# The FFN down product of three layers by Strassen's seven block products, with the weight sums made on chip

## The chip, the cores and the metric

The kernel runs on all 8 cores of one Trainium2 chip. Each core computes half of one sequence of the batch (4 sequences of 8192 tokens). The metric is the device time in microseconds (us) of the slowest core. Most executions of one kernel agree within 0.3%. In some executions, whatever the kernel, one die (cores 0 to 3 or 4 to 7) or both are granted a lower TensorE clock and the time is several per cent longer. Those runs are called slow here, they are left out of every comparison, and where only one die was slow I also read the undisturbed die of the same run.

Names used below: PE is the matmul engine (TensorE), DVE is VectorE, ACT is ScalarE, POOL is GpSimd, SP is the engine that issues most plain DMAs. The "casting queue" is the DMA queue fed by GpSimd, which loads fp32 weights and writes them as bf16; the profile calls it q0 software_dynamic. The "hardware queue" is the one fed by SP, q1 hardware_dynamic; it copies without casting.

## The reference, cut to what matters

```python
def swiglu(h, w_gate, w_up, w_down):
    return (jax.nn.silu(h @ w_gate) * (h @ w_up)) @ w_down      # 1024 -> 2816 -> 1024

for i in range(4):                                   # DEPTH
    h = rmsnorm(x, mix_pre_g[i])
    m = mixer_a(h, ...) if i % 2 == 0 else mixer_b(h, ...)   # gMLP, pooling
    x = x + rmsnorm(m, mix_post_g[i])
    h = rmsnorm(x, ffn_pre_g[i])
    f = swiglu(h, ffn_w_gate[i], ffn_w_up[i], ffn_w_down[i])
    x = x + rmsnorm(f, ffn_post_g[i])
```

Input, output and weights are fp32. The kernel multiplies in bf16.

## The kernel before

A core goes through its tokens in 5 tiles of two halves (512, 400 or 384 tokens). Within a tile it runs the four layers, each a mixer and an FFN. While one half is in a vector phase (norms), the other half keeps PE busy. Programs for the engines are made by a list scheduler: each operation is a task with buffers that it reads and writes, and with a priority; each engine then executes its tasks strictly in the order that the scheduler chose.

All weights pass through one ring of six 1 MB slots. Cast weights come over the casting queue; one weight of mixer B (`w2_s`, folded on chip in tile 0 and stored as bf16) comes over the hardware queue.

```python
NSLOT = 6
class Piece:                       # one slot of the weight ring
    def __init__(self, src, cast=True, reads=(), k=None, parts=1):
        eng = "pool" if cast else "sp"
        ...
        t = t_dma(eng, (0, seq[0]), slot, src, list(reads), [var], ...)
        if last_load[0] is not None:
            t.preds[last_load[0]] = -1.0       # loads keep their order
...
BIG = [sb("BIG%d" % h, [128, 32 * HW[h]], BF16) for h in range(2)]
WSM = sb("WSM", [128, 1024], BF16)             # mixer A's constants: buffers of their own
BIAS = sb("BIAS", [128, 2048], F32)
w2_s = dram("w2_s", [2, 8, 128, 1024], BF16, "Internal")
...
def out_proj(s, v, loc, nk, rhs_fn, st, base, together=0, pr=None):
    for oc in range(KC):                       # 8 groups of 128 output channels
        b = bs[oc]                             # one PSUM bank each
        for i in range(0, nk, 8):
            mm_group(...)                      # nk matmuls of the half's width
        post_evac(st, v, s, oc, b)             # ACT: square for the norm, copy to MS
    st.rstd()                                  # statistics: squares summed on DVE,
                                               # one matmul with ONESM, Ln and Exp on ACT
...
# mixer B
pcs = [Piece(wb_in[j, q]) for q in range(2)]
tp = [Piece(w2_s[j].rearrange("k p n -> p k n")[:, :, q * 512:(q + 1) * 512], cast=False,
            reads=[("w2_s", j, kb) for kb in range(8)], k=8) for q in range(2)]
...
# mixer A
if t > 0:
    load_bias(j, s)                            # BIAS and WSM from DRAM, hardware queue
...
# FFN
pcs = [Piece(wf_gu[l, q]) for q in range(11)]
for pi in range(11):
    for h in hs:
        ffn_head(s, vout[h], pi, pcs[pi])      # gate, up, silu, product
tp = [Piece(wf_dn[l, q]) for q in range(6)]
for h in hs2:
    out_proj(s, v, by_block(tp, NJ), NJ, lambda k, v=v: bigfm(v, 0, k), st, 0)
    chain(v, s, st, gpost, nxt[h], ...)        # norm, residual, next norm -> H
```

## Time and profile before

| | before |
|---|---|
| time, median of 3 runs | 5720.78 us (5720.65 to 6790.34; the last is a slow run) |
| undisturbed die, by core | 5714.0 to 5718.3 us, granted clock 0.998 to 0.999 |
| PE busy on the profiled core | 5696.8 of 5754.8 us |
| PE idle between matmuls, median core | 20 us in tile 0, 16 in tiles 1 to 4 |
| time lost to half clock, median core | 9.5 us |

The last two rows are worked out from the trace: the idle time is the sum of all stretches between the first and the last matmul in which no matmul runs; the half-clock loss is half the time that the record of the granted clock shows at 0.5, whether PE had work in it or not. Tile 0 is taken to end at 1090 us.

The spans by core and their granted clock, before:

```profile
core 5: 5718.3 us, clock 0.998
...
die 0 (median of its cores): 5747.7 us, clock 0.992
die 1 (median of its cores): 5716.1 us, clock 0.999
```

Die 0 was slightly disturbed in this execution (stretches at 0.81), so the undisturbed die 1 is the yardstick: about 5716.

The groups of matmuls by shape on core 6, before. The number in front of the bar is the count; behind it come busy time, then the mean length of one (which overlaps its neighbours, so cost per matmul is busy time over count), then the idle time just before them:

```profile
L499 PE MATMUL ps<-BIG,WR 128*128 128x384 bf16 x7312 | 1208.4, 326 | 2.5 <-ACT SQ L480 0.8
```

That is 1208.4 / 7312 = 165 ns for a matmul of width 384, and hardly any waiting. What PE waited for on core 6, before (total us, times, longest):

```profile
PE ps L499 <- DVE SQF L601: 17.0, 7, 13.6
PE ps L499 <- DVE ACC L596: 7.4, 1, 7.4
PE ps L499 <- DVE H L641: 5.8, 5, 2.5
```

The longest of these are at the very start. Mixer weights and FFN weights don't appear in it (apart from 3.2 us for another mixer weight): in the kernel before, PE practically never waits for a DMA.

The timeline of PE and DVE-fed statistics at the hand-over from layer 2's FFN to layer 3's mixer B in tile 1, core 5 before (start, us, engine, line, operation, count, idle before):

```profile
2074.80 8.58 PE L499 MATMUL ps<-BIG,WR 128*128 128x512 bf16 x39
2083.22 2.97 PE L499 MATMUL ps<-WR,H 128*128 128x512 bf16 x13
2086.03 0.38 PE L499 MATMUL ps<-SQF,ONESM 128*128 128x512 bf16 x1
...
2095.75 8.44 PE L499 MATMUL ps<-BIG,WR 128*128 128x384 bf16 x48
...
2107.96 4.26 PE L499 MATMUL ps<-WR,H 128*128 128x512 bf16 x19 [0.82 <-DVE H L641]
```

The down product of the second half ends at 2083.3; its statistics matmul follows 2.7 us later; the mixer's output product, which uses `w2_s`, starts at 2095.75 without a wait; and the next half's input is ready 0.8 us late.

### The profile page before, as it was taken

Reading aid. Unit: us, or ns where it says so; the run is one execution under the profiler, and the core shown is the slowest. Engines: PE = TensorE matmul, PEld = TensorE weight load, DVE = VectorE, ACT = ScalarE, POOL = GpSimd, SP = SyncE. Lnnn points to the kernel's source line nnn. Section 1 sums busy time; section 2 is a strip of 40 time slices with the busy share of each in tenths; the row PEclk is TensorE's granted clock in tenths of the full one; section 3 lists DMA queues with packets and bytes.
Section 4 is the critical chain, followed back from the end, with each engine's and each line's share of the span. In section 5 each row is a group of like instructions: output and inputs, shape, how many; then the busy total and the mean of one; then the engine's idle time right before and its main releaser. Section 6 shows DMA issues by size and latency. Waiting matters only on the chain.

```text
span 5754.8 us, 92936 instructions; the slowest of 8 cores (5714.0 to 5754.8 us)
## 1 busy us (share of the span) xinstructions
PE 5696.8 (99%) x33311; PEld 3157.3 (55%) x33311; DVE 2630.8 (46%) x4841; ACT 2432.9 (42%) x5236; POOL 258.7 (4%) x492
## 2 busy tenths in 40 slices
PE   8999999999999999999999999999999999999999
PEld 4555555555555555555545555555565555555556
DVE  5453536352625454443436253524454444525352
ACT  5352635352525353533354253524534453525252
POOL 0000000000000000000000000000000000000000
PEclk9999999999999999999999999999999999999999
DMA  7856676664445545754544455655554676455544
GB/s 141 141 97 107 114 127 117 123 130 81 80 89 98 96 88 107 142 95 81 93 85 86 91 112 111 122 111 103 103 105 95 119 140 112 89 92 96 107 88 90
DMA packets 131409, 604.39 MB, mean 105 GB/s; under 512 B 12560, under 2 KB 55952, under 8 KB 67600
## 3 DMA queue, kind: packets, MB, share of 16 engines
q0 software_dynamic: 70272, 507.82, 51.1%
q1 hardware_dynamic: 60688, 90.63, 5.2%
q8 instruction: 276, 4.52, 0.3%
q14 instruction: 173, 1.42, 0.1%
HBM read 1082.53 MB, written 23.66 MB: 192 GB/s over the span
## 4 chain that ended last, share of the span: by engine, by line
PE 94%; DVE 2%; DMA 1%; ACT 1%; issue 1%; another core or an unknown queue 0%; DVEq 0%; SPq 0%; ACTq 0%; POOLq 0%
PE ps L499 94%; DMA MS<-xT 1%; DVE ACC L596 1%; DVE H L641 0%; DVE MS L688 0%; DMA WR<-wb_out 0%; ACT RS L622 0%; ACT BIG L480 0%; ACT RS L624 0%; DVE BIG L833 0%; DVE X L694 0%; ACT SQ L480 0%; DVE ACC L593 0%; ACT MS L480 0%; DMA X<-xT 0%
## 5 line engine op out<-in xcount | busy, mean ns | idle before, releaser
L499 PE MATMUL ps<-H,WR 128*128 128x384 bf16 (+2 forms) x16640 | 2967.7, 338 | 11.8 <-ACT SQ L480 4.3
L499 PEld LDWEIGHTS ps<-H,WR 128*128 128x128 bf16 x16640 | 1617.7, 98 | 1254.6 <-issue 24.7
L499 PE MATMUL ps<-BIG,WR 128*128 128x384 bf16 (+4 forms) x11056 | 1941.5, 337 | 2.1
L499 PEld LDWEIGHTS ps<-BIG,WR 128*128 128x128 bf16 x11056 | 1078.4, 98 | 832.8 <-issue 24.2
L750 DVE TENSOR_TENSOR BIG<-ps,SG 128x384 bf16<-128x384 f32 (+2 forms) x880 | 510.0, 585 | 1374.3 <-PE ps L499 1294.7
L480 ACT ACTIVATE SG<-ps 128x384 bf16<-128x384 f32 (+2 forms) x880 | 442.8, 513 | 1553.1 <-PE ps L499 1540.7
L596 DVE TENSOR_TENSOR ACC<-ACC,SQ 128x384 f32<-128x384 f32 (+2 forms) x730 | 428.7, 587 | 770.0 <-ACT SQ L480 706.7
L499 PE MATMUL ps<-WR,H 128*128 128x512 bf16 x3216 | 728.3, 386 | 12.8 <-DVE ACC L596 8.1
L480 ACT ACTIVATE MS<-ps 128x384 f32<-128x384 f32 (+3 forms) x648 | 324.5, 511 | 958.8 <-PE ps L499 947.6
L480 ACT ACTIVATE BIG<-ps 128x512 bf16<-128x512 f32 (+1 forms) x914 | 477.3, 561 | 338.2 <-PE ps L499 335.1
L499 PEld LDWEIGHTS ps<-WR,H 128*128 128x128 bf16 x3216 | 318.5, 99 | 402.7 <-issue 67.7
L688 DVE TENSOR_TENSOR MS<-MS,RS 128x384 f32<-128x384 f32 (+3 forms) x640 | 364.6, 580 | 200.0 <-ACT RS L624 199.9
L641 DVE SCALAR_TENSOR_TENSOR H<-X,GV,RS 128x384 bf16<-128x384 f32 (+2 forms) x576 | 330.0, 643 | 142.8 <-ACT RS L624 142.8
L480 ACT ACTIVATE SQ<-X 128x384 bf16<-128x384 f32 (+2 forms) x576 | 300.5, 549 | 200.9 <-DVE ACC L593 96.6
L694 DVE SCALAR_TENSOR_TENSOR X<-MS,GV,X 128x384 f32<-128x384 f32 (+2 forms) x560 | 354.6, 642 | 0.0
L480 ACT ACTIVATE SQ<-ps 128x384 bf16<-128x384 f32 (+3 forms) x648 | 321.9, 510 | 46.2 <-DVE ACC L596 29.2
L509 POOL DMA_DIRECT2D WR<-wf_gu x220 | 116.1, 528 | 2485.1 <-PE ps L499 2452.6
L593 DVE TENSOR_TENSOR ACC<-SQ 128x384 f32<-128x384 bf16 (+2 forms) x146 | 85.4, 585 | 189.4 <-ACT SQ L480 188.6
L480 ACT ACTIVATE SQ<-BIG 128x512 bf16<-128x512 bf16 x268 | 168.2, 638 | 7.1
L622 ACT ACTIVATE RS<-ps,EPSC 128x384 f32<-128x384 f32 (+2 forms) x152 | 92.6, 609 | 139.2 <-PE ps L499 139.1
L864 DVE SCALAR_TENSOR_TENSOR ACC<-ps,GV,BIAS 128x384 f32<-128x384 f32 (+2 forms) x184 | 107.5, 587 | 57.9 <-PE ps L499 54.8
L480 ACT ACT_TABLE_LOAD x94 | 120.6, 1283 | 19.7 <-PE ps L499 14.1
(63 smaller groups left out, 1555.9 us busy)
## 6 DMA issues: line engine op xcount, KB each, us to landing
WR<-wf_gu POOLq DMA_DIRECT2D x220, 1024.0 KB, 10.5
WR<-wf_dn POOLq DMA_DIRECT2D x120, 1024.0 KB, 9.0
WR<-wa_in POOLq DMA_DIRECT2D x79, 1024.0 KB, 14.3
WR<-wa_out POOLq DMA_DIRECT2D x40, 1024.0 KB, 10.0
WR<-wb_in POOLq DMA_DIRECT2D x20, 1024.0 KB, 10.1
WR<-w_s SPq DMA_DIRECT2D x20, 1024.0 KB, 10.2
yT<-MS SPq DMA_DIRECT2D x56, 192.0 KB, 16.6
X<-xT SPq DMA_DIRECT2D x48, 192.0 KB, 18.5
```

The costliest lines, as they stand in the source:

```text
L480: return e.activation(out=out() if callable(out) else out, in_=in_() if callable(in_) else in_, func=func, **kw)
L499: return e.matmul(out(), lhsT=lhsT() if callable(lhsT) else lhsT, rhs=rhs() if callable(rhs) else rhs, start=start, stop=stop)
L509: return e.dma_start(out=out() if callable(out) else out, in_=in_)
L593: t_dve(self.prio + (1,), lambda e: e.tensor_tensor(out=acc, in0=o0(), in1=o(), op=ALU.add), [k0, kq], ka, v.n)
L596: d = t_dve(self.prio + (1,), lambda e: e.tensor_tensor(out=acc, in0=acc, in1=o(), op=ALU.add), [kq] + ka, ka, v.n)
L622: t.insts.append((lambda e: e.activation(out=r, in_=bank(b, 0, v.n), func=AF.Ln, bias=EPSC[:]), [b, ("EPSC",)], kr, d_act(v.n)))
L641: t_dve(CH + (s, v.p, 1), lambda e, o=o, a=a, g=g, r=r: e.scalar_tensor_tensor(out=o, in0=a, scalar=g, in1=r, op0=ALU.mult, op1=ALU.mult), ...
L688: t_dve(CH + (s, v.p, 0), lambda e: e.tensor_tensor(out=m, in0=m, in1=r, op=ALU.mult), kf("MS", v, fc) + kr, kf("MS", v, fc), v.n)
L694: t_dve(CH + (s, v.p, 0), lambda e: e.scalar_tensor_tensor(out=o, in0=m, scalar=g, in1=x, op0=ALU.mult, op1=ALU.add), kf("MS", v, fc) + kf ...
L750: t_dve((0, s, v.p), lambda e, o=o, sg=sg, bu=bu: e.tensor_tensor(out=o, in0=bank(bu, 0, v.n), in1=sg(), op=ALU.mult), [bu, ksg], ko, v.n)
L864: t_dve((0, s, v.p, 0), lambda e, b=b, o3=o3, bb=bb, lg=lg, x0=x0, nl=nl, n=n: e.scalar_tensor_tensor(out=o3, in0=bank(b, x0 - v.c0, nl * ...
```

## The change

The intent: in layers 0 to 2 of tiles 1 to 4, do the down product [tokens x 2816] @ [2816 x 1024] as a 2x2x2 block product by Strassen's scheme, with seven half-size block products in place of eight. Each matmul then has half the width (192, 200 or 256 tokens), and there are 308 of them per half in place of 176. The seven combinations of weight blocks are made once, in tile 0, by DVE from the bf16 pieces that are in the ring anyway, and stored as bf16 in DRAM (`dn_s`); later tiles load them over the hardware queue. The token-side combinations are made by DVE after each gate/up piece. The last layer, and tile 0, keep the plain product (with its blocks in another order).

The diff, cut to its core:

```diff
+AB = (0, 22272)
+FB = (0, 19712)
+EXT = 16384
...
-    BIG = [sb("BIG%d" % h, [128, 32 * HW[h]], BF16) for h in range(2)]
+    BIGA = sb("BIG", [128, AB[1] + 32 * WB], BF16)         # one buffer for both halves
...
-    NSQ, NSG = 3, 3
+    NSQ, NSG, NT = 3, 4, 3
+    TB = [sb("TB%d" % i, [128, 512], F32) for i in range(NT)]
-    WSM = sb("WSM", [128, 1024], BF16)
-    BIAS = sb("BIAS", [128, 2048], F32)
+    BIAS = BIGA[:, EXT:EXT + 4096].bitcast(F32)            # now lies in the FFN's region
+    WSM = BIGA[:, EXT + 4096:EXT + 5120]
+    dn_s = dram("dn_s", [3, 2, 128, 154 * 128], BF16, "Internal")
...
+    def g_sums(s, v, kk):                                  # token-side sums, per gate/up piece
+        t_dve(pr, ... garr(v, 0, kk, 1) + garr(v, 4, kk, 1) ...)
+        t_dve(pr, ... garr(v, 4, kk, 1) - garr(v, 1, kk, -1) ...)
+        t_dve(pr, ... garr(v, 0, kk) + garr(v, 1, kk) ...)
...
+    def down7(s, v, gp, st7, st, rank, last):              # one group of outputs, one half
+        m4 = z.product(pr + (0, 0), z.q, m, unit(0, 0, 10), rg(5), True, alloc=z.pq)
+        z.product(pr + (0, 1), z.q, m, unit(0, 10), rg(5), False)
+        z.m4_taken((0, s, v.p, 0), m)                      # ACT copy PSUM -> TB
+        z.product(pr + (1,), z.p, m, unit(1), rg(4), True).preds.setdefault(m4, 0.0)
+        z.add_to_t((0, s, v.p, 0), z.p, m)                 # DVE: TB += PSUM
+        z.product(pr + (2,), z.r, m, unit(2), rg(6), True, alloc=z.r)
+        z.add_to_t((0, s, v.p, 0), z.r, m)
+        z.product(pr + (3,), z.q, m, unit(3), rg(0), False)   # then ACT copy to MS
+        z.product(pr + (4,), z.p, m, unit(4), rg(1), False)   # then ACT copy to MS
+        z.product(pr + (5,), z.q, m, unit(5), rg(2), False)   # then MS = TB - PSUM, two squares
+        z.product(pr + (6,), z.p, m, unit(6), rg(3), False)   # then MS = TB - PSUM, two squares
...
+    def stage(s, l, jobs, claimed):                        # tile 0: the weight sums
+        for fn, n, src, dsts in jobs:                      # 5 per piece of wf_dn
+            t = Task("dve", (1, s))
+            t.alloc = var                                  # one of five staging buffers in BIG
+            ...
+            for c0, nn, dst, key in dsts:
+                t_dma("sp", (0, s), dst, ...)              # store to dn_s
...
+            if keep:                                       # t > 0 and l < 3
+                dn7 = [Stream(dn_s[l, g], 154, ...) for g in (0, 1, 0)]
+                for rank, (i, g, last) in enumerate(((0, 0, False), (0, 1, True), (1, 1, False), (1, 0, True))):
+                    down7(s, vlast[h], g, dn7[(0, 1, 1, 2)[rank]], sts[h], rank, last)
+            else:
+                ...                                        # plain product, as before
+                if t == 0 and l < 3:
+                    for q in range(6):
+                        setup_dn(s, l, q, tp[q], claimed)
```

`BIAS` and `WSM` lose their own buffers, because the extra token-side arrays need the room. The cut also leaves out four further parts of the change: the scheduler's model of DMA time (one shared server for both queues in place of one for each), `dynamic_dma_scratch_size=8192` in the program's set-up, another order of blocks in the plain down product that is kept, and the loss of a separate buffer (`SQF`) for the last sum of the statistics.

## The prediction

> **What bounds the kernel now.** TensorE. The page shows PE busy 5697 of 5755 us (99%), the chain that ended last is 94% PE, the granted clock was 0.99 to 1.00 on all cores. PE waits total 58 us, some 25 at the start. Only PE work removed, or PE waits added, moves the time; DVE (46%), ACT (42%) and DMA have room.
>
> **Removed.** The FFN down product of tiles 1 to 4 in layers 0 to 2: 12 sub-layers of two halves, 176 matmuls per half. The groups by shape give PE time per matmul: 221 ns at width 512, 172 at 400, 167 at 384, 110.8 at 256, 64 at 144. Strassen does 308 matmuls per half at half the width. The narrow ones of the last sub-layer (256, 144) run almost in proportion, so I interpolate 84 ns at 192, 87 at 200. Per half: 512: 39.0 -> 34.1 us; 400: 30.3 -> 26.7; 384: 29.3 -> 25.9. Per layer: two halves of 512, one of 400, five of 384; in all 91 us, 1.6%. An ideal 7/8 would be 95; the rest is the fixed cost of 3168 more matmuls. The Trainium skill, "TensorE: Matmul & The Clock Gate", section "Wait — 56ns, not 53.3ns?", states about 2.5 ns each, an estimated 8 us; the trace roughly agrees (110.8 at 256, 106.7 of it streaming).
>
> **Added.** (a) DVE: three bf16 sums per gate/up piece and half, an estimated 0.7 to 1.3 us, under 12.4 us of PE work: off the path. (b) Evacuation: per output group two additions and two subtractions on DVE (0.55 to 0.69 us each), three copies on ACT (0.5 to 0.6). While the second half projects at 384, DVE has the first half's chain, 18.7 us, plus 9 for combining and statistics, against 25.9 us of PE; before it was 23 against 29. So that chain ends about when PE needs H, and the second half's starts behind: I expect 10 to 20 us of PE wait in all, most in tiles 3 and 4. (c) DMA: 15.1 MB of bf16 per down stage for 6.3 MB cast from fp32. 8 KB packets took 322 ns on the hardware queue (407 GB/s over 16 engines), 636 on the casting queue. A 1 MB piece needs an estimated 2.6 us, PE eats one in 2.7 to 3.5, six slots give about a quarter-stage of lead: no lasting stall. (d) Tile 0: 90 DVE sums (an estimated 0.6 us each) and 30 MB of stores; slots are held longer: 0 to 8 us.
>
> **Critical path.** 5721 - 91 + 15 (waits) + 4 (tile 0) = **5649 us**, range **5622 to 5690**. Chances: faster by over 2% (below 5606) 0.03, since even the ideal is 95 us; within 2% 0.94; slower 0.03.
>
> **What would show it.** Groups by shape: 7392 matmuls of width 192, 200, 256 at 84, 87, 111 ns, 4224 wide ones fewer; PE busy about 5606. Waits: PE for DVE H and for ACT or DVE evacuations up by 10 to 20 us, none large for DMA. Hardware queue about 300 MB, casting queue about 430. Granted clock unchanged.
>
> **What would make it wrong.** PE stalls at the products of 22 matmuls (1.8 us) because evacuations are late: 336 products, 0.2 us each would be 67 us. Weights arriving late, because one group's five pieces hold five of six slots for two quarters. Denser weight loads lowering the granted clock.

## More of the kernel before

`w2_s` is read with `[:, :, q*512:(q+1)*512]`, so each partition's 8 KB come as eight separate rows of 1 KB. And `BIAS` has a buffer of its own, so its load can be issued at almost any time.

The page of the profiled execution of the kernel before (its core 1), whole lines from the parts on engines, queues, the chain that ended last, and DMA issues (count, KB each, median us from issue to landing):

```profile
span 5754.8 us, 92936 instructions; the slowest of 8 cores (5714.0 to 5754.8 us)
...
PE 5696.8 (99%) x33311; PEld 3157.3 (55%) x33311; DVE 2630.8 (46%) x4841; ACT 2432.9 (42%) x5236; POOL 258.7 (4%) x492
...
q0 software_dynamic: 70272, 507.82, 51.1%
q1 hardware_dynamic: 60688, 90.63, 5.2%
...
PE 94%; DVE 2%; DMA 1%; ACT 1%; issue 1%; another core or an unknown queue 0%; DVEq 0%; SPq 0%; ACTq 0%; POOLq 0%
...
WR<-w_s SPq DMA_DIRECT2D x20, 1024.0 KB, 10.2
```

PE is busy 99% of the span, and the chain that ended last is PE for 94%. Nothing else is near its limit. The queue lines give packets, MB and the share of the 16 DMA engines' time.

## The result, and the profile after

| | before | after |
|---|---|---|
| median of the 5 runs | 5721.86 us (5720.65 to 6790.34) | 5809.21 us (5785.89 to 6701.45) |
| fast runs | 5720.65, 5720.78, 5721.86 | 5809.21, 5792.50, 5785.89 |
| after over before | | 1.0131, 95% interval 1.0105 to 1.0157 |

A ratio here and below is the mean time of one kernel's fast runs over the mean of the other's fast runs of the same rounds, so it isn't quite the ratio of the medians quoted. The change is correct, and it costs 1.3%: inside the 2% band, but outside the predicted range and on the other side.

The same lines of the page, after (its core 6, the slowest):

```profile
span 5807.7 us, 99963 instructions; the slowest of 8 cores (5745.1 to 5807.7 us)
...
PE 5599.6 (96%) x36271; PEld 3372.2 (58%) x36479; DVE 2999.6 (52%) x5915; ACT 2424.7 (42%) x5192; POOL 220.2 (4%) x420
...
q0 software_dynamic: 59904, 432.32, 43.5%
q1 hardware_dynamic: 107776, 302.60, 15.6%
...
PE 83%; DMA 8%; ACT 3%; DVE 3%; issue 2%; SPq 0%; another core or an unknown queue 0%; DVEq 0%; ACTq 0%; POOL 0%; POOLq 0%
...
WR<-w_s SPq DMA_DIRECT2D x20, 1024.0 KB, 27.6
```

The PE work did shrink, and the bytes moved as forecast. But the chain that ended last has lost 11 points of PE and gained 7 of DMA, and `w_s` (the same 20 loads of the same megabyte, by a line that the change does not touch) takes 27.6 us to land in place of 10.2.

The spans by core, after:

```profile
core 6: 5807.7 us, clock 0.990
...
die 0 (median of its cores): 5752.4 us, clock 0.994
die 1 (median of its cores): 5784.3 us, clock 0.991
```

The groups of matmuls by shape on core 6, after:

```profile
L540 PE MATMUL ps<-BIG,WR 128*128 128x384 bf16 x4672 | 788.1, 330 | 58.2 <-DMA WR<-w_s 42.0 <-DVE BIG L827 8.1 <-ACT SQ L521 5.7
...
L540 PE MATMUL ps<-BIG,WR 128*128 128x192 bf16 x4620 | 386.0, 246 | 0.8 <-DMA WR<-dn_s 0.5 <-ACT MS L521 0.4
...
L540 PE MATMUL ps<-BIG,WR 128*128 128x256 bf16 x2024 | 225.2, 273 | 0.0
```

A width of 192 costs 386.0 / 4620 = 83.5 ns, 256 costs 111.3 ns; with the 81.3 us of width 200, and without the 19.5 us of the 176 matmuls of width 256 that were there before, the new product costs 386.0 + 225.2 + 81.3 - 19.5 = 673 us. The forecast was 673. And these matmuls hardly wait. The 58.2 us are in front of a *different* product, the plain ones of width 384.

What PE waited for on core 6, after:

```profile
PE ps L540 <- DMA WR<-w_s: 42.0, 7, 7.3
PE ps L540 <- ACT SG L521: 26.1, 17, 12.4
PE ps L540 <- DVE H L688: 23.7, 13, 2.9
...
PE ps L540 <- DVE SQ L644: 17.8, 9, 13.4
PE ps L540 <- DVE BIG L827: 15.5, 6, 6.4
```

Three new waits: for `w_s`; for a silu result (`SG`) or the product of it (`BIG L827`), which is the gate/up stage; and for `H`, the next stage's input.

**The sum.** On the median core of each (of the undisturbed die, for before):

| us | before | after |
|---|---|---|
| PE busy (the rest) | 5655 | 5602 |
| PE idle between matmuls | 35 | 131 |
| before the first and after the last matmul | 26 | 27 |
| span | 5716 | 5760 |
| half-clock loss, as defined above | 9.5 | 35.5 |
| of it, while PE was busy | 3 | 21 |

Idle time rose by 96 us. Busy time should have fallen by 91 and fell by 53. Of these missing 38 us, 18 went to matmuls at half clock; the rest of the half-clock loss falls on stretches in which PE had nothing to do, where it costs nothing more. A matmul that stands alone after a gap shows its whole length of some 326 ns, not the 165 that it adds in a row, and the busy time lies in some 170 pieces after and some 80 before: an estimated 90 x 0.16 = 14 us. About 6 us are not traced. The cores also spread: core 6 has 181 us idle and a half-clock loss of 59.5 us (30 while PE was busy), and the slowest core is what is timed. About 12 of its 181 us are probably not real: on cores 0 and 6 some 200 matmul records are missing (the page counts 36271 matmuls and 36479 weight loads), and in the kernel before these two cores show 25 and 28 us in tiles 1 to 4 where the others show 12 to 16.

**Where the clock goes.** After a gap of some microseconds the granted clock is mostly 0.5 for 3.4 us or more. The windows on core 6 after, at the hand-over to layer 3's mixer B in tile 1 (window, length, then busy time and count of PE, PEld, DVE, ACT, POOL, then granted clock, DMA share, GB/s):

```profile
2120.00:2130.00 10.00, 9.78 (x82) 5.34 (x81) 7.32 (x12) 7.29 (x15) 0.00 (x0) 1.00 0.99 169
2130.00:2138.00 8.00, 0.90 (x11) 0.53 (x8) 7.14 (x12) 4.24 (x10) 0.00 (x0) 0.76 1.01 285
2138.00:2145.00 7.00, 7.00 (x36) 3.83 (x35) 0.32 (x1) 0.92 (x3) 0.00 (x0) 0.79 0.07 22
```

In the second window PE is idle for 7 us while all 16 DMA engines are busy; in the third PE runs 36 matmuls in 7.00 us, 194 ns each in place of 165, because the clock was granted at half speed for part of it. A 7 us gap costs 7 us, and then some more. The Trainium skill, "TensorE: Matmul & The Clock Gate", section "What's actually happening", says that an idle window of about 3.4 us takes the clock to half. The trace agrees on the unit: the 17 stretches on core 6 (118.9 us in all) last 3.41, 6.83 or 10.24 us, but for the one at the end. It does not agree that only gaps of that length count: on the eight cores, 58 of the 66 gaps over 3.4 us were followed by such a stretch, but so were 37 of the 104 gaps of 1.7 to 3.4 us, and 3 of the 154 of 0.8 to 1.7 us.

**Cause 1: a load in small packets, beside casts.** The chain on core 6 after, around the same place (start, us, what):

```profile
2107.58 29.67 DMA WR<-w_s
```

The load of `w_s` was issued at 2107.58 and took 29.67 us. PE had nothing to do from 2130.3 on and started when it landed:

```profile
2137.38 12.29 PE L540 MATMUL ps<-BIG,WR 128*128 128x384 bf16 x64 [7.10 <-DMA WR<-w_s]
2152.56 7.71 PE L540 MATMUL ps<-WR,H 128*128 128x512 bf16 x35 [2.88 <-DVE H L688]
```

(That is core 6's timeline of PE; the second line is a cause that comes further down.) Why 29.67 us? I counted the records of single DMA packets on core 6 in both traces, at this hand-over, where two loads of `w_s` make 2048 packets of 1 KB:

| core 6 | window, us | 1 KB packets, hardware queue | 8 KB packets, casting queue |
|---|---|---|---|
| before | 2063 to 2071 | 306 | 128 |
| before | 2071 to 2080 | 1742 | 0 |
| after | 2116 to 2132 | 357 | 299 |
| after | 2132 to 2138 | 1533 | 33 |

As long as casts are queued, the small packets go at about one for each cast packet, and hardly move; once the casts have run out, 1533 of them are through in 6 us. The Trainium skill, "DMA: Bandwidth & Descriptors", section "Queues, rings and completion order", says that each DMA engine takes turns between the queues that have work, packet by packet; the 357 to 299 agree, if each record of the trace is one such packet (the page's packet can hold several descriptors). A queue with 1 KB packets beside one with 8 KB packets then gets about an eighth of the bytes: here 357 KB of 2749. In the kernel before, this load was issued 30 us ahead of its use (2063.69 for 2093.24) with one cast beside it. After, it is issued 23 us ahead (2107.58 for 2130.3), and four casts and the load of `BIAS` (issued at 2105.17) are in flight with it. Why the issue comes later I did not test; the last load of `dn_s`, in front of it in the ring's order, is issued only at 2097.86.

**Cause 2: `BIAS` now loads at the hand-over.** Its memory lies in the FFN's region, so its load can't be issued before the last changed FFN of a tile is over. That is exactly where `w_s` is wanted, on the same queue, and `BIAS` goes first: from 2108 to 2116 us the hardware queue moved 125 packets of 8 KB and only 21 of 1 KB.

**Cause 3: the sums of tile 0 stop DVE.** DVE's timeline in tile 0 on core 6 after, and the PE line that follows from it:

```profile
282.30 0.57 DVE L827 TENSOR_TENSOR BIG<-ps,SG 128x400 bf16<-128x400 f32 x1 [2.15 <-PE ps L540]
299.38 0.69 DVE L978 TENSOR_TENSOR BIG<-WR 128x1024 bf16<-128x1024 bf16 x1 [16.51 <-DMA dn_s<-BIG]
...
301.84 0.57 DVE L827 TENSOR_TENSOR BIG<-ps,SG 128x400 bf16<-128x400 f32 x1
```

```profile
303.15 5.05 PE L540 MATMUL ps<-BIG,WR 128*128 128x400 bf16 x15 [7.64 <-ACT SG L521]
```

L978 is a weight sum. It waits 16.51 us for its staging buffer, whose store to `dn_s` (packets of 2 KB on the hardware queue, beside casts) hasn't landed. Behind it in DVE's order stands L827, the last product of the gate/up stage, which was ready all the time; PE waits for it. "DVE has room" (52% busy) is true and beside the point: an engine that runs in order stops at its first unready instruction. On core 6 the sums waited 66.5 us in all.

**Cause 4: a longer tail at the hand-over.** The groups end with a subtraction and two squares at once, where the plain product ended with one square. This is in the 23.7 us of waits for `H`; E1 below shows it undisturbed.

**Cause 5: the prefetch of the next tile's tokens** also comes in small packets (1.5 KB) on the hardware queue. After tile 0 the slowest of its loads took 34 to 47 us to land, by core, and some cores show a gap of PE there, of up to 12.4 us (at most 3.9 in one piece before). The landing itself isn't new: in the kernel before, the slowest took 42 to 52 us. What the change took away is the time that they had; why, I did not trace.

### The profile page after: what moved, and what is told of

Same layout as the page of the kernel before. It is cut to its first block, busy times and chain, and to the rows that moved or that the text cites. A ratio compares the mean times of both kernels' runs of the same rounds, so it can differ in the third digit from the quotient of the medians.

```text
span 5807.7 us, 99963 instructions; the slowest of 8 cores (5745.1 to 5807.7 us)
## 1 busy us (share of the span) xinstructions
PE 5599.6 (96%) x36271; PEld 3372.2 (58%) x36479; DVE 2999.6 (52%) x5915; ACT 2424.7 (42%) x5192; POOL 220.2 (4%) x420
## 3 DMA queue, kind: packets, MB, share of 16 engines
q0 software_dynamic: 59904, 432.32, 43.5%
q1 hardware_dynamic: 107776, 302.60, 15.6%
## 4 chain that ended last, share of the span: by engine, by line
PE 83%; DMA 8%; ACT 3%; DVE 3%; issue 2%; SPq 0%; another core or an unknown queue 0%; DVEq 0%; ACTq 0%; POOL 0%; POOLq 0%
PE ps L540 83%; DMA WR<-w_s 3%; DMA dn_s<-BIG 2%; DMA MS<-xT 1%; DVE H L688 1%; DMA WR<-wa_in 1%; ACT BIG L521 1%; ACT SQ L521 1%; ACT RS L666 1%; DMA WR<-wf_dn 1%; ACT L521 0%; DVE MS L736 0%; ACT RS L668 0%; DVE ACC L638 0%; ACT L651 0%
## 5 line engine op out<-in xcount | busy, mean ns | idle before, releaser
L540 PE MATMUL ps<-BIG,WR 128*128 128x384 bf16 (+5 forms) x14196 | 1850.5, 292 | 69.0 <-DMA WR<-w_s 42.0
L540 PEld LDWEIGHTS ps<-BIG,WR 128*128 128x128 bf16 x14224 | 1304.8, 98 | 590.6 <-issue 103.0
L540 PE MATMUL ps<-WR,H 128*128 128x512 bf16 x3142 | 711.6, 382 | 48.6 <-DVE H L688 20.4
L521 ACT ACTIVATE MS<-ps 128x384 f32<-128x384 f32 (+4 forms) x552 | 274.0, 509 | 766.2 <-PE ps L540 760.7
L736 DVE TENSOR_TENSOR MS<-MS,RS 128x384 f32<-128x384 f32 (+3 forms) x640 | 362.6, 577 | 174.9 <-ACT RS L668 174.7
L827 DVE TENSOR_TENSOR BIG<-ps,SG 128x384 bf16<-128x384 f32 (+2 forms) x352 | 199.3, 573 | 455.6 <-PE ps L540 402.2
L742 DVE SCALAR_TENSOR_TENSOR X<-MS,GV,X 128x384 f32<-128x384 f32 (+2 forms) x560 | 352.7, 637 | 0.0
L521 ACT ACTIVATE SQ<-ps 128x384 bf16<-128x384 f32 (+4 forms) x456 | 221.5, 505 | 52.0 <-DVE ACC L638 33.5
L521 ACT ACTIVATE SQ<-MS 128x384 bf16<-128x384 f32 (+2 forms) x256 | 130.7, 545 | 144.9 <-DVE MS L912 73.8
## 6 DMA issues: line engine op xcount, KB each, us to landing
WR<-w_s SPq DMA_DIRECT2D x20, 1024.0 KB, 27.6
```

What stands on the lines that cost most here:

```text
L521: return e.activation(out=out() if callable(out) else out, in_=in_() if callable(in_) else in_, func=func, **kw)
L540: return e.matmul(out(), lhsT=lhsT() if callable(lhsT) else lhsT, rhs=rhs() if callable(rhs) else rhs, start=start, stop=stop, skip_group_ ...
L736: t_dve(CH + (s, v.p, 0), lambda e: e.tensor_tensor(out=m, in0=m, in1=r, op=ALU.mult), kf("MS", v, fc) + kr, kf("MS", v, fc), v.n)
L742: t_dve(CH + (s, v.p, 0), lambda e: e.scalar_tensor_tensor(out=o, in0=m, scalar=g, in1=x, op0=ALU.mult, op1=ALU.add), kf("MS", v, fc) + kf ...
L827: t_dve((0, s, v.p), lambda e, o=o, sg=sg, bu=bu: e.tensor_tensor(out=o, in0=bank(bu, 0, v.n), in1=sg(), op=ALU.mult), [bu, ksg], ko, v.n)
```

## The experiments

My theory: the time went to waits that the change makes *outside* the new product (causes 1 to 5), multiplied by the clock. The rival, from the prediction: DVE has too much to do in the new product and falls behind. A second rival: the loads of `dn_s`, 3.3 times the traffic on the hardware queue, disturb everything else.

Eighteen runs in five groups; each group ran on one chip beside the kernel before. The kernel before measured 5718.97 to 5725.45 us in its fast runs, but for three that were mildly disturbed (5746 to 5778). Three edits recur, so I name them.

Edit R ("rows"): the layout of `w2_s`, so that a load has rows of 8 KB. Same bytes, same order of work.

```diff
-    w2_s = dram("w2_s", [2, 8, 128, 1024], BF16, "Internal")
+    w2_s = dram("w2_s", [2, 2, 128, 4096], BF16, "Internal")
-            const_dma(w2_s[j, kb], so, ...)
+            const_dma(w2_s[j].rearrange("q p (k n) -> p k q n", k=8)[:, kb], so.rearrange("p (q n) -> p q n", q=2), ...)
-            tp = [Piece(w2_s[j].rearrange("k p n -> p k n")[:, :, q * 512:(q + 1) * 512], cast=False, ..., k=8) ...]
+            tp = [Piece(w2_s[j, q], cast=False, reads=[...]) for q in range(2)]
```

Edit B ("bias later"): `load_bias` waits for a point inside the next stage, and so is issued behind `w_s`.

```diff
-    def load_bias(j, s):
-        t_dma("sp", (1, s), BIAS, bias_s[j], [("bias_s", j)], KBIAS, ...)
+    def load_bias(j, s, gate):
+        t_dma("sp", (1, s), BIAS, bias_s[j], [("bias_s", j)] + gate, KBIAS, ...)
-            if t > 0:
-                load_bias(j, s)
+            if t > 0 and l == 0:
+                load_bias(j, s, blocks(1, 5 * HW[1], 128))
+                ...                     # l > 0: after the second block of mixer A
```

Edit T ("short tail"): for the half whose statistics are on the path, the last two squares go straight to PE, which adds them up in PSUM, in place of two more additions on DVE.

```diff
+            if self.split and i >= KC - 3:
+                if i == KC - 3:
+                    d = t_dve(..., acc + square, ...)
+                    self.sum = Var("pss")
+                t_pe(..., [(bank(b), ONESM[:], o, i == KC - 3, last, ...)], ...)
+                return
+                        split=kind == 1 and t > 0 and l < 3 and v.p == 1)
```

### The change again, unedited (after_again)

> The changed kernel itself, unaltered, on the chip of this call, so that the edits beside it have a partner of the same rounds. Both theories: about 1.3% over before (5785 to 5810 us), TensorE idle 115 to 180 us per core, 24 to 48 us of it before the 384-wide matmuls on BIG and WR, half-clock time 65 to 120 us per core.

Measured: correct, 4 fast runs of 5789.95 to 5809.53 us, ratio 1.011 [1.0054, 1.0167]; `w_s` landed in 25.7 us; idle on the median core 37.5 us in tile 0 and 97.5 in tiles 1 to 4. The result holds on another chip.

### E1: edit R alone (e1_w2_rows)

> Only the layout of w2_s in DRAM: rows of 8 KB per partition in place of eight rows of 1 KB; the order of all instructions is the same. Theory (the small packets of the hardware queue take turns, one for one, with the 8 KB packets of the casting queue): landing of the w_s loads falls from 27.6 us (median) to about 12, the TensorE idle before the 384-wide matmuls on BIG and WR falls from 24-48 us per core to under 10, and with the half-clock stretches behind those gaps the time falls by 30 to 60 us against the changed kernel. Rival (the loads are issued too late because the slots come free late, or the bandwidth of the memory is used up): landing stays above 20 us and the time moves by less than 10 us.

Measured: correct, fast runs 5752.09, 5759.89 and 5765.55 us; ratio 1.0034 [0.9947, 1.0121]. The interval is wide because the kernel before had two mildly disturbed runs in this group; read against the undisturbed 5719 it is 0.6 to 0.8% longer. `w_s` in E1's DMA issues:

```profile
WR<-w_s SPq DMA_DIRECT2D x20, 1024.0 KB, 17.4
```

And the group of width 384 in E1, core 6, which had 58.2 us of idle time in front of it:

```profile
L540 PE MATMUL ps<-BIG,WR 128*128 128x384 bf16 x4672 | 774.6, 327 | 9.8 <-ACT SG L521 5.6 <-ACT BIG L521 3.7
```

The wait for `w_s` is gone from it altogether, with nothing changed but the layout of `w2_s` and with it the size of a packet (the traces of core 1 show every engine's instructions in the same order), and the time fell by some 40 us (mean of the fast runs 5800 to 5759). By core, the median landing was 23.3 to 27.8 us in the change and is 12.1 to 17.4 us here. That confirms cause 1. It also speaks against the second rival: the traffic of `dn_s` is all still there. `w_s` still takes longer than in the kernel before (7.9 to 10.2 us by core): `BIAS` is still in front of it.

E1 lets cause 4 be seen alone. PE, DVE and ACT at the same hand-over, E1, core 2:

```profile
2102.86 9.77 PE L540 MATMUL ps<-BIG,WR 128*128 128x256 bf16 x88
...
2112.73 0.69 DVE L918 TENSOR_TENSOR MS<-TB,ps 128x512 f32<-128x512 f32 x1
...
2113.52 1.15 ACT L521 ACTIVATE SQ<-MS 128x512 bf16<-128x512 f32 x2 [1.18 <-DVE MS L918]
...
2116.56 0.38 PE L540 MATMUL ps<-SQ,ONESM 128*128 128x512 bf16 x1
```

The last product ends at about 2112.5 (where the matmuls on `WR,H` begin), the statistics matmul comes at 2116.56: 4.1 us later, in place of 2.7. The subtraction (0.69), two squares (1.15) and the additions behind them stand in a row. PE's wait for `H` at this hand-over is 2.67 us here, 0.82 before.

### E2: hold the sums back until the gate/up stage is over (e2_stage_gate)

```diff
+                    gate = [k for h in hs for f in (NJ // 2 - 1, NJ - 1) for k in bigfm(vout[h], 0, f)[1]]
-                        setup_dn(s, l, q, tp[q], claimed)
+                        setup_dn(s, l, q, tp[q], claimed, gate)     # every sum and store reads gate
```

> Only in tile 0: the weight sums and the stores of their operands wait until both halves have finished gate and up, when no casting load competes. Theory (in tile 0 a sum at the head of the in-order DVE queue waits for a staging buffer whose store is held up by casts, and the silu product behind it is late): the gaps of TensorE of 6 to 8 us at about 295, 512 and 863 us vanish, DVE waits for dn_s stores fall from 66 us to under 20, cores 4 to 7 gain 15 to 35 us, cores 0 to 3 5 to 15, and the time falls by 10 to 30 us. Rival (tile 0 is slow because of the added DVE work and store bytes as such, whenever they run): the gaps move later and the time stays within 8 us.

Measured: correct; one fast run, 5835.76 us; five slow. In the slow ones the undisturbed dies had medians of 5782 to 5820 us, against 5754 to 5776 for the change. The gaps in front of the down product were gone, but a new one, of 17 to 19 us on four of the cores, stood in front of a statistics matmul of tile 0: the sums now stopped DVE in the middle of the norm. It failed. The block moved, to a place where what stands behind it is more urgent.

### E3: E1 and E2 together (e3_both)

> Both edits. Theory: the gains add, 45 to 85 us against the changed kernel, so 5710 to 5750 us, about equal to before; what is left then is DVE's backlog (waits for H and SQ at the hand-over of the halves). Rival of both: no change.

Measured: correct, fast runs 5780.95, 5784.19 and 5803.70 us, ratio 1.0093 [1.0023, 1.0162]: slower than E1. Edit R still gave its part (`w_s` landed in 17.3 us), E2's gate took it back (idle time in tile 0 61.5 us, 47 in E1).

### E4: edit R, without the additions to TB (e4_no_t_adds; result wrong)

```diff
-        z.add_to_t((0, s, v.p, 0), z.p, m)
-        z.add_to_t((0, s, v.p, 0), z.r, m)
```

> On top of the 8 KB rows for w2_s; wrong on purpose: the two additions to T per output group (M1 and M2 after M4) are left out, 96 operations on DVE of 0.55 to 0.69 us, 54 to 60 us of DVE time in all, 4.5 to 5.5 per down stage. They come early in each group, so the length of the tail after the last product is as before. Theory (DVE's backlog makes the hand-over gaps of tiles 1 to 4): TensorE idle in tiles 1 to 4 falls from 70-90 us to under 50 us, the time by 20 us or more. Rival (the gaps come from the longer tail: the last product, then a subtraction, two squares, two additions, then the chain): idle changes by less than 10 us.

Measured: wrong result, as meant (relative error 0.71); fast runs 5767.22 and 5774.83 us; idle time in tiles 1 to 4 on the median core 72 us, 70.5 in E1. Half of the DVE work of each group's combination is gone (two of its four operations), and the idle time is the same. This refutes the first rival, which is the prediction's term (b): DVE is not behind because it has too much to do.

### E5: edit R, with the statistics of the changed FFN summed by PE (e5_pe_stats)

```diff
-        ... pe=s % 4 == 2 and v.p == 0 and max(w.n for w in vlast.values()) <= 400)
+        ... pe=s % 4 == 2 and v.p == 0 and max(w.n for w in vlast.values()) <= 400
+                        or kind == 1 and t > 0 and l < 3)
```

> On top of the 8 KB rows; correct: in the twelve changed sub-layers the squares of the down output are summed by TensorE (a matmul with ones each) in place of DVE. DVE loses 192 additions (about 110 us), the tail gets shorter by one to two DVE operations; TensorE gains 168 matmuls (about 30 us). Both DVE theories: hand-over idle in tiles 1 to 4 falls by 30 us or more, so the time stays about equal or falls by up to 20 us. If neither DVE load nor the tail matters: time rises by 30 us.

Measured: correct; one fast run, 5780.89 us. Idle time in tiles 1 to 4 fell from 70.5 to 50 us; as E4 took DVE work away without this, the tail (cause 4) is real. But all eight squares of each half now cost PE a matmul, an estimated 30 us in all (some 7 more matmuls of 0.17 to 0.22 us for each of two halves in 12 FFNs), and no time was gained. Edit T was made from this: only the last two squares, only one half.

### E6: edit R, no sums (e6_no_sums; result wrong)

```diff
+        for o, (jj, kh) in ((2, (0, 0)), (3, (1, 0)), (4, (0, 1)), (5, (1, 1)), (6, (0, 1))):
+            for c0, nn, d, key in to(o):
+                t_dma("sp", (0, s), d, ...)         # store a block as it is, straight from the ring
+        return
```

> On top of the 8 KB rows; wrong on purpose: in tile 0 the five sums of each weight piece are not made, unsummed quarters are stored in their place straight from the slot. Same bytes and packets of the stores, no DVE sums and no staging buffers. Theory (a sum that waits for a staging buffer at the head of DVE's queue holds up the silu products): the gaps at about 295, 511 and 856 us vanish, idle in tile 0 falls by 15 to 25 us on the cores that have them, time by 15 to 35 us. Rival (the store traffic itself slows the weights): the gaps stay or turn into waits for weight loads.

Measured: wrong result, as meant (relative error 0.87); fast runs 5760.58 and 5778.54 us, ratio 1.0081 [1.0043, 1.0119]. The dies that ran undisturbed (median clock of the die 0.990 or more), slow runs included, were at 5721 to 5756 us, median 5730; E1's at 5728 to 5747, median 5741. Idle time in tile 0 on the median core fell from 47 to 29 us. The same bytes are stored, only DVE's part is missing: so cause 3 is worth some 18 us of idle time in tile 0. The profiled execution was a slow one, but on its undisturbed die the four cores show 27 to 34 us too, where E1's eight cores show 32 to 58. The fast times show no gain over E1, which two runs can't settle; the dies show some 11 us, under the 15 expected at least. Idle time in tiles 1 to 4, where no sum is made, went the other way, from 70.5 to 80 us, which nothing here explains.

### E7: edit R, sums held back and at lower priority (e7_gate_low)

```diff
-            t = Task("dve", (1, s))
+            t = Task("dve", (2, s))                 # and the gate of E2
```

> Both edits of before (8 KB rows; sums of tile 0 after gate and up), with the sums now ranked behind the chain of the finished half. Theory (the earlier gated version lost because sums of 0.7 us stood ahead of statistics and chain): its gaps of 15 to 25 us before the statistics matmul in tile 0 fall below 8 us and the time is 10 to 30 us under the 8 KB rows alone, 5725 to 5755 us. Rival (sums that wait for a staging buffer block DVE wherever they stand): no gain.

Measured: correct; fast runs 5773.91 and 5814.10 us. In part it did what was expected: the gap in front of the statistics matmul is 6.4 to 9.3 us (up to 19.1 in E2), and a sum waits at most 6.3 us for its buffer, although stores in its chain took 15.22 and 21.38 us to land. But another gap of 8.6 us stands further on, on every core, idle time in tile 0 is 51 us (47 in E1), and no time was gained. The explanation is argued, not shown: priority decides only the order that the scheduler writes down, from its own idea of when a store lands; once written, an in-order engine has no priorities.

### E8: edits R and B (e8_bias_later)

> On top of the 8 KB rows; correct: the load of BIAS and WSM (1.25 MB), which the change moved to the hand-over of layers because their buffer now lies under the FFN's, waits for a product of layer 3's gate and up (for layer 0) or for the second V piece (for layer 2). Theory (that load stands in front of w_s on the hardware queue and takes turns with wb_in and wa_in): w_s lands in under 14 us (17.4 before), TensorE's waits for wb_in and wa_in weights fall by 5 to 10 us per core, time by 5 to 20 us. Rival (the weights are late because slots come free late): no change over 5 us.

Measured: correct; one fast run, 5758.34 us, six slow; the eight undisturbed dies were at 5719 to 5743 us, median 5728, where E1's median is 5741. `w_s`:

```profile
WR<-w_s SPq DMA_DIRECT2D x20, 1024.0 KB, 12.7
```

12.7 in place of 17.4 us on the profiled cores; by core the medians are 11.0 to 13.3 us (12.1 to 17.4 in E1), and the longest single loads 16.2 to 18.8 us (24.4 to 26.7). That confirms cause 2, at about 10 us on a die.

### E9: edit R, the sums on GpSimd (e9_pool_sums)

```diff
-            t = Task("dve", (1, s))
+            t = Task("pool", (1, s))
```

> On top of the 8 KB rows; correct: the five sums per weight piece of tile 0 run on GpSimd, not on DVE[...]. Theory (a sum waiting for a staging buffer blocks DVE): the gaps at about 295, 511 and 856 us vanish as in the run without sums, idle of tile 0 falls from 47 us (median core) to about 30, half-clock loss by 10 us, time by 15 to 35 us. Rival (GpSimd's queue, blocked in the same way, delays the casting loads it also issues): tile 0 shows waits for WR instead and no gain.

Measured: correct, fast runs 5798.05 to 5801.70 us, ratio 1.014 [1.0097, 1.0184]: as slow as the change itself, E1's gain lost. GpSimd's sums, and DVE beside them, in the timeline of E9, core 4:

```profile
335.97 2.49 DVE L736 TENSOR_TENSOR MS<-MS,RS 128x400 f32<-128x400 f32 x1
...
343.21 11.63 DVE L742 SCALAR_TENSOR_TENSOR X<-MS,GV,X 128x400 f32<-128x400 f32 x1
...
354.76 0.56 DVE L736 TENSOR_TENSOR MS<-MS,RS 128x400 f32<-128x400 f32 x1
```

L736 takes 0.56 us when GpSimd is quiet and 2.49 while it sums; one L742 took 11.63 us. One sum takes GpSimd 2.25 us (0.69 on DVE). The Trainium skill, "SBUF — State Buffer", section "SBUF: two separate sides", says that DVE and GpSimd share a pair of ports, that it is an exclusive lock for a whole instruction, and that a DVE instruction with two SBUF inputs is among those that are blocked. The trace agrees: 2.49 us is about one GpSimd sum of waiting. It failed: DVE's queue was freed, and its two-input instructions then ran at a quarter of their speed. Idle time in tile 0 rose from 47 to 72 us, most of it in front of statistics matmuls (68.3 us on core 4, the start included). It also rose in tiles 1 to 4, from 70.5 to 85 us, where no sum is made; that is not explained.

### E10: edits R and T (e10_short_tail)

> On top of the 8 KB rows; correct: in the second half of the twelve changed sub-layers only the last two squares go to TensorE's statistics sum directly, not through two DVE additions (24 more matmuls of ones, about 5 us). The time from the last down matmul to the end of the statistics falls from 4.1 us to about 3. Theory (the longer tail makes the hand-over gaps): idle of tiles 1 to 4 falls from 70 us (median core) by 10 to 20 us, half-clock loss somewhat, time by 5 to 20 us. Rival: idle unchanged, time up by 5 us.

Measured: correct; one fast run, 5751.79 us, five slow; the six undisturbed dies were at 5728 to 5741 us, median 5735, which is within the spread of E1's; idle time in tiles 1 to 4 59 us, 70.5 in E1. The idle time confirms cause 4; in the time it is too small to see.

### E11: edits R, B and T with the sums on GpSimd (e11_all)

> All four edits: 8 KB rows for w2_s, bias load later, sums on GpSimd, short tail. If the theories hold the gains add: idle of tile 0 about 30 us, of tiles 1 to 4 about 45, half-clock loss about 20, time 5690 to 5720 us on an undisturbed chip, a little under before.

Measured: correct, fast runs 5779.83 and 5780.74 us, ratio 1.0106 [1.0062, 1.0149]. E9's loss outweighs the three repairs together.

### E12: edits R, B and T (e12_three)

> Three edits: 8 KB rows for w2_s, BIAS load later, short tail; correct. If they add: cores of an undisturbed die 5710 to 5725 us (before 5715, 8 KB rows alone about 5740), idle of tiles 1 to 4 about 50 us. If BIAS and tail did nothing: 5735 to 5745.

Measured: correct, fast runs 5734.06, 5744.14 and 5751.64 us, ratio 1.0032 [1.001, 1.0053]. The three repairs add up: from 1.3% to 0.3%. Idle time in tiles 1 to 4 is 49.5 us (94 in the change), but in tile 0 it is 50.

### E13: E12, with the stores of the sums on the casting queue (e13_store_pool)

```diff
-                t_dma("sp", (0, s), dst, lambda unit=unit, c0=c0, nn=nn: unit()[:, c0:c0 + nn], ...)
+                t_dma("pool", (0, s), dst, lambda unit=unit, c0=c0, nn=nn: unit()[:, c0:c0 + nn], ...)
```

> The three edits, and the stores of the sums go through the casting queue; correct. If taking turns between the two queues is what makes the stores slow: a store lands in 10 to 15 us where it took 25 to 40, DVE's waits for dn_s stores fall below 20 us, tile 0 idle falls to about 30 us, 10 to 20 us less than with the three edits alone. Rival: the casts issued behind stores that wait for sums come late, tile 0 idle stays at 45 us or rises.

Measured: correct, fast runs 5719.98 to 5727.78 us, ratio 1.0006 [0.999, 1.0021]: a tie with the kernel before, 1.2% better than the change. The stores no longer compete packet by packet with casts; they stand in line with them. What the sums waited for, on core 6, in the change and here:

```profile
DVE BIG L978 <- DMA dn_s<-BIG: 66.5, 18, 16.5
...
DVE BIG L989 <- DMA dn_s<-BIG: 66.1, 37, 9.3
```

So the waits did not get less in all, as was expected (under 20 us): 66.1 us in 37 waits, in place of 66.5 in 18. What fell is the longest one, 9.3 us in place of 16.5 (18.2 in E12). The stores show the same: from E12 to E13, on core 6, the median landing of a sum's store rose from 5.2 to 9.9 us, and the longest fell from 35.4 to 25.2 us. Idle time on the median core: 38 us in tile 0, 52.5 in tiles 1 to 4, half-clock loss 22.

What PE still waits for in E13, core 6:

```profile
PE ps L540 <- DVE SQ L655: 22.3, 9, 13.0
PE ps L540 <- ACT BIG L521: 18.5, 40, 1.0
PE ps L540 <- DVE H L699: 16.2, 9, 3.5
```

No `w_s`. The first is mostly the start (13.0 at once, as before). The rest are many small ones.

### E14: E12, with the scheduler told that stores land 15 us later (e14_store_late)

```diff
-                      128 * nn * 2, (csem[kind], var))
+                      128 * nn * 2, (csem[kind], var)).tail = 15.0
```

> The three edits, and the plan that fixes the order of instructions is told that a store of sums lands 15 us later than it thought; correct. If the order (a sum placed before a silu product in the belief that its buffer is free) is the cause: the gaps at 295, 511 and 856 us vanish, but the pieces are held longer and waits for wb_in or wa_in weights may appear at the start of the next layers of tile 0; tile 0 idle 25 to 45 us. Rival: no change.

Measured: correct, fast runs 5746.33 to 5765.77 us, ratio 1.0063 [1.0047, 1.0079]; idle time in tile 0 59 us, more than E12's 50. It failed. The sums' waits for stores did fall (26.0 us on core 4, 71.4 in E12), but every core has a new gap of 21 to 25 us in tile 0. That the later plan puts the sums in front of work that matters is an argument; the gap was not followed to its cause.

### E15: E12 without the sums (e15_bound; result wrong)

The edit of E6 on E12.

> The three edits without the sums of tile 0 (unsummed quarters are stored); wrong on purpose. A bound for what any better placing of the sums can reach: cores of an undisturbed die 5695 to 5710 us, 0.1 to 0.3% under before. If it isn't under before, the hand-over of tiles 1 to 4 alone eats the saving.

Measured: wrong result (relative error 0.87); fast runs 5716.91 to 5722.25 us, ratio 0.9997 [0.998, 1.0015]. This is about the floor of what tile 0 can still give: with the sums free, the change would only tie. The median core is at 5707.5 us, 8 below the kernel before.

### E16: E13, with the prefetch of tokens on the casting queue too (e16_prefetch_pool)

```diff
-            t = t_dma("sp", (1, s, p, fc), a, xT3[:, fc, tok0:tok0 + n], gate, ka, ...)
+            t = t_dma("pool", (1, s, p, fc), a, xT3[:, fc, tok0:tok0 + n], gate, ka, ...)
```

> e13_store_pool and the prefetch of x through the casting queue; correct. If taking turns is the cause: the eight prefetch loads land in 20 us or less (47 before), the gap of 12 us at about 1035 us vanishes, tile 0 idle falls to about 27 us, time 5705 to 5722 us, 0.0 to 0.25% under the kernel before. Rival: the loads of weights behind them come late, time as e13 or above.

Measured: correct, fast runs 5724.49 to 5730.91 us, ratio 0.9998 [0.9958, 1.0039]; against the undisturbed fast runs of before in this group (5722.44 to 5725.45) it is a tie. The slowest load of the prefetch after tile 0 lands in 17.1 to 23.7 us, by core, where it had taken 35 to 48 in E13, the gap of 12 us is gone, and idle time in tile 0 is 29 us on the median core. That confirms cause 5: the gap hangs on these loads. But the time is E13's: in tiles 1 to 4 the idle time rose from 52.5 to 64 us, where the prefetch now stands in front of mixer weights in the casting queue (core 6 waits 21.9 us for `wa_in`, 7.7 in E13).

### E17: the kernel before with edit R (e17_before_rows)

> The kernel before with only the 8 KB rows of w2_s. Expected: no change, within 0.1% (5715 to 5725 us on an undisturbed chip), since its w_s loads (10.2 us) were waited for by nothing. If it gains 0.3% or more, the rows are a gain of their own and not a repair of what the change did.

Measured: correct, fast runs 5721.93 and 5723.04 us, ratio 0.9988 [0.9937, 1.0039]; idle times as before (22 and 16 us). A control: in the kernel before, the small packets cost nothing, because the load had time. Edit R repairs something that the change made matter; it isn't a gain of its own.

## Why the prediction was wrong, point by point

Right:

- PE is what bounds the kernel before, and the cost of the new product: 673 us forecast and measured (83.5, 88.0 and 111.3 ns per matmul, forecast 84, 87 and 111). The Trainium skill's 2.5 ns for each further matmul ("TensorE: Matmul & The Clock Gate", section "Wait — 56ns, not 53.3ns?") fitted the interpolation.
- The traffic: 302.60 and 432.32 MB, forecast 300 and 430. Waits for `dn_s` itself: 0.5 us. PE busy on the page: 5599.6 us, forecast 5606, though the nearness is partly luck (matmuls at half clock are in it, and some 200 records of that core are missing).
- None of the three dangers that it named came true: the products of 22 matmuls did not stall for their evacuations, the new weights were not late, and the denser weight loads did not lower the clock by themselves (the clock records of this execution show full and half, and no step between).

Wrong: the term "15 (waits) + 4 (tile 0)" of the sum. Measured on the median core, it was 96 us of idle time (75 to 80 in tiles 1 to 4, 19 in tile 0), 18 us of matmuls at half clock and an estimated 14 us behind the gaps, and more on the slowest core, which is the one that is timed. The steps of it:

- "(b) ... I expect 10 to 20 us of PE wait in all": the mechanism was a DVE that has too much to do. E4 took half of that work away and nothing changed. What is true in it is only the end of each half, where subtraction and two squares come in a row (2.7 to 4.1 us; E10).
- "(c) ... no lasting stall": worked out for the loads that the change adds, and right for them. What stalled was a load that the change does not touch, `w_s`, because it comes in 1 KB packets and now meets casts (E1: gone with larger rows). I had costed bytes per second for each queue, and not who takes turns with whom. The cost of a load that waits its turn was missing, and it is the largest one shown: E1, which repairs it, is some 40 us faster.
- "(d) ... 0 to 8 us" for tile 0: the sums were costed by their own length, "90 sums, 0.6 us each". The cost is the wait of the first one for a buffer, with the gate/up product behind it in the same queue (E6, E13).
- Missing: `BIAS` under the FFN's region, which I had read in the diff as a saving of memory. It moves a 1 MB load to the worst moment (E8).
- Missing: the clock. I wrote "granted clock unchanged", from the clock of a kernel that has no gaps. A gap that a change adds can be paid again, in part, at half clock.
- Missing: the slowest core. The change's cores spread over 5745 to 5808 us, where before's undisturbed ones lie within 4.3 us in the profiled execution, and within 17 in its other undisturbed runs.

What the repairs show: with rows of 8 KB, `BIAS` later, a shorter tail and the stores on the casting queue (E13), the change ties with the kernel before, and its median core is some 7 us ahead of it (5709 against 5716). No version beat both kernels clearly. Of the 91 us, E13 pays some 55 back as idle time (90 us in place of 35 on the median core) and 9 as matmuls at half clock (12 in place of 3); an estimated 11 lie behind its gaps (some 150 pieces of busy time in place of 80), and an estimated 5 are the further statistics matmuls of edit T. The lead of the median core is what is left, and the spread of its cores (5686.1 to 5726.2 us) takes it, as the slowest one is timed.

Open: why neighbouring cores of the repaired versions differ by some 20 us (in E13, cores 0 and 2 are at 5723.9 and 5710.8, cores 1 and 3 at 5703.2 and 5686.1); and how much of the landing times is contention between cores for memory, which no run here separates. The four parts of the change that the cut leaves out are in every repaired version, so what they cost or gain is open too. And E6's gain shows in idle time and on undisturbed dies, not in its fast times.

## What to carry to other kernels

When PE is 99% busy, a change that removes PE work is worth what it removes less every gap it opens anywhere, and a gap of some microseconds is often charged again at half clock; so look for the work that the change *moves* (a load whose buffer is now shared, a store that holds a buffer, an instruction at the head of an in-order queue), above all where the diff looks like housekeeping. Give a DMA that shares the engines with 8 KB casting packets rows of 8 KB too: the same megabyte took 23.3 to 27.8 us in 1 KB packets, by core, and 11.0 to 17.4 us in 8 KB ones. Putting it in the same queue as the casts helps only against the longest waits: the stores' median landing rose (E13). And judge slack by lead time, not by the share of busy time: the small packets had been there all along, and were harmless while the load had 30 us (E17).

## What the Trainium skill lacked or had wrong

- "DMA: Bandwidth & Descriptors", section "Queues, rings and completion order", says that an engine takes turns between queues packet by packet, but draws no consequence for two queues with packets of unlike size. Here a plain load in 1 KB packets got 357 packets through while casts in 8 KB packets got 299, so 1 MB took 27.6 us beside casts and 17.4 us in rows of 8 KB. Stores in 2 KB packets made DVE wait up to 17.4 us for a buffer, and token loads in 1.5 KB packets took up to 47 us (up to 24 on the casting queue).
- "TensorE: Matmul & The Clock Gate", callout "Peak-current limiter: 13/16 clock" in section "Seeing it yourself", advises to budget 1.95 GHz for dense matmuls on all cores. Here all 8 cores ran matmuls 99% of the time at a granted clock of 0.997 to 0.999 in every undisturbed run of the kernel before. The page's 13/16 does occur: the disturbed die of the kernel before has stretches at 0.8125, and in slow runs the mean on a die fell to 0.82. That state was frequent (7 of 9 runs of the kernel before in one group, 2 of 7 in another) but not the rule. Both states have to be budgeted, and compared apart.
- The same page, section "What's actually happening", gives an idle window of about 3.4 us for half clock; the stretches here have that unit, but 37 of 104 gaps of only 1.7 to 3.4 us were followed by one too. The cost in a kernel with scattered gaps isn't given: here 17 stretches, 118.9 us at half clock on one core, for 181 us of idle time.
- "GPSIMD Engine Reference", section 3.1, gives 1.96 for a GpSimd addition against DVE's at fp32 (N = 2048). For bf16 at 1024 columns it was 2250 ns against 690 ns here, 3.3 times.
- "SBUF — State Buffer", section "SBUF: two separate sides": its exclusive lock agrees with 0.56 us growing to 2.49 us. One instruction took 11.63 us, about five GpSimd sums of 2.25 us; the page doesn't say whether the loser of the lock can lose several turns, and no run here settles it.
